# Two modulation vectors by one-column products on TensorE in the opening of a two-block network, with the small vectors loaded ahead on the same queue

## The chip, the cores and the metric

The kernel runs on one core of a Trainium2 chip, in one launch. The metric is the device time of that launch in microseconds (us): the median of the runs shown, 2753.62 us for the kernel before (3 runs, 2752.54 to 2756.70 us).

## The reference, cut to what matters

The first block has two layers, each of attention and a gated feed-forward part, over 1024 tokens of width 1024; a second block follows. Every layer of the first block is modulated by six vectors made from a condition `c`:

```
cond = jax.nn.silu(c)                                   # 1 x 1024
mod = (cond @ ada_w[i] + ada_b[i])                      # 1 x 6144, float32
sh1, sc1, g1, sh2, sc2, g2 = jnp.split(mod, 6, axis=-1)
h = rmsnorm(x, norm_mix[i]) * (1 + sc1) + sh1
y = windowed_gqa(h, a_w_in[j], a_w_out[j], a_sink[j])   # begins with h @ a_w_in
```

For layer 0, `sc1` (vector 1) and `sh1` (vector 0) are needed before the first product `h @ a_w_in`. Each is a product of the 1024 values of `cond` with a 1024 x 1024 block of `ada_w`, 4.2 MB in float32. The change concerns how these two are made; nothing else of the reference is touched.

## The kernel before, in words

Activations are kept transposed: 128 features on the partitions, 512 tokens (a half, `hf`) along the free side, eight feature tiles `j`. A 1024-wide vector lies as 128 partitions x 8 columns.

The opening is written out in `build` (L1961 onwards). `load_vectors` loads nine small vectors: eight go as rows into two buffers through ACT's queue (L207), are transposed on PE (L210) and copied by DVE (L212); the attention sink goes by ACT's queue as well (L239). `cond` is made from the first (L232 to L236). SP's queue then loads, in program order, four 512 KB tiles of x (first half, L303), eight 512 KB blocks of the weights of vector 1 (`w1`, L259), four tiles of x (second half), eight blocks of the weights of vector 0 (`w0`), and after them the first two column blocks of `a_w_in` (three transfers at L544, 512 KB of memory for each block, of which the first is cut in two pieces of 64 columns). The spills of x to memory (L321, eight of 512 KB) and the third column block follow.

On the engines other than SP the order inside `with net.in_order()` is that of the program text, for each engine by itself. For PE it is: 32 transposes of x's first half (`turn_x`, L312), the spreading of the reciprocal norms of that half over 128 partitions (`spread`, L389), the finish of vector 1 (`ada_fin`, eight transposes, L281), 32 transposes of the second half, its spreading, the finish of vector 0, and then the first product of the attention's projection (`project_first`, L590 to L592), which is outside the `with`. ACT squares the rows of x (L494), copies the transposes out of PSUM (L314), and makes the high part of h (`hh`, L527), with vector 0 as its bias. DVE makes the modulation vectors: `ada_acc` runs over the eight blocks of a vector and adds `block * cond[:, k]` to a 128 x 1024 sum (L269 for the first block, L271 for seven); then `ada_fin` transposes the sum on PE and DVE adds up each group of 128 (L282) and adds the bias (L283). DVE also makes the reciprocal square roots by a chain of tiny operations (`rstd_steps`, L335 to L342), scales x by norm and vector 1 (`nu`, L516), and makes the low part of h (`hl`, L530). For vector 0 the program weaves the steps of `ada_acc` with the reciprocal roots of the second half. The two column blocks of `a_w_in` are split into a high part by ACT (L536) and a low part by POOL (L537).

A product of two float32 operands (not rounded to the PE's one-pass format) shows as two LDWEIGHTS and two MATMULs in the trace: `col_sums` (L378) issues four one-column products for each sum, and eight instructions appear for them; `spread` issues four, and eight appear. A transpose shows as one.

Of the kernel before, what the change touches and what calls it, by code (L numbers as in the profile page):

```python
# [15 lines left out]
AX = mybir.AxisListType  # L16

P = 128
L = 1024
D = 1024  # L20
KT = D // P
# [127 lines left out]
class Net:  # L149
# [49 lines left out]
    def load_vectors(self):  # L199
        nc, I = self.nc, self.I  # L200

        def rows(specs, name):
            n = sum(r for _, r in specs)
            raw = self.slab("tmp", shape=(P, 1024))
            at = 0
            for ap, r in specs:
                nc.scalar.dma_start(raw[at:at + r, 0:P], ap)  # L207
                at += r
            ps = self.bank("r")
            nc.tensor.transpose(ps[:, 0:n], raw[0:n, 0:P], self.ident[0:n, 0:n])  # L210
            col = self.cst([P, n], name)
            nc.vector.tensor_copy(col, ps[:, 0:n])  # L212
            return col

        v1 = rows([(I["c"].rearrange("b (r p) -> (b r) p", p=P), 8),
                   (I["ada_b"].rearrange("l (r p) -> (l r) p", p=P), 96)], "v1")
        v2 = rows([(I["norm_mix"].rearrange("l (r p) -> (l r) p", p=P), 16),
                   (I["norm_ffn"].rearrange("l (r p) -> (l r) p", p=P), 16),
                   (I["final_norm"].rearrange("(r p) -> r p", p=P), 8),
                   (I["norm_gain_2"].rearrange("l (r p) -> (l r) p", p=P), 8),  # L220
                   (I["conv_w_2"].rearrange("l k (r p) -> (l k r) p", p=P), 12),
                   (I["b_glu_2"].rearrange("l (r p) -> (l r) p", p=P), 4)], "v2")
        self.c_col = v1[:, 0:8]
        self.adab = v1[:, 8:104]
        self.nmix = v2[:, 0:16]
        self.nffn = v2[:, 16:32]
        self.fnorm = v2[:, 32:40]
        self.ngain2 = v2[:, 40:48]
        self.convw = v2[:, 48:60]
        self.bglu = v2[:, 60:64]  # L230
        th = self.small([P, 8], "cth", 1)
        nc.scalar.activation(th, self.c_col, AF.Tanh, scale=0.5)  # L232
        self.cond = self.cst([P, 8], "cond")
        t2 = self.small([P, 8], "cth2", 1)
        nc.vector.scalar_tensor_tensor(t2, th, 1.0, self.c_col, op0=ALU.add, op1=ALU.mult)
        nc.vector.tensor_scalar_mul(self.cond, t2, 0.5)  # L236
        self.mod = {}
        sinkb = self.cst([P, 16], "sinkb")
        nc.scalar.dma_start(sinkb, I["a_sink"].to_broadcast([P, 16]))  # L239
        self.sink8 = self.cst([P, 16], "sink8")  # L240
        nc.vector.tensor_scalar_mul(self.sink8, sinkb, 8.0)
# [32 lines left out]
    def ada_fin(self, i, v, acc):  # L274
        nc = self.nc
        col = self.cst([P, 8], f"mod{i}_{v}")
        red = self.small([P, 8], "adar")
        for hf in range(2):
            ps = self.bank(self.ada_tag, shape=(P, 4, P))
            for j in range(4):  # L280
                nc.tensor.transpose(ps[:, j, :], acc[:, (hf * 4 + j) * P:(hf * 4 + j + 1) * P], self.ident)  # L281
            nc.vector.reduce_sum(red[:, hf * 4:(hf + 1) * 4], ps, axis=AX.X)  # L282
        nc.vector.tensor_add(col, red, self.adab[:, i * 48 + v * 8:i * 48 + v * 8 + 8])  # L283
        self.mod[i, v] = col
        return col

    def ada_scale(self, i, v, gain):
        col = self.mod[i, v]
        s = self.cst([P, 8], f"sc{i}_{v}")
        self.nc.vector.scalar_tensor_tensor(s, col, 1.0, gain, op0=ALU.add, op1=ALU.mult)  # L290
        return s
# [1669 lines left out]
def build(tc, I, out, dbg=None, stop=None):  # L1961
    with ExitStack() as ctx:
        net, nc = Net(tc, I, out, dbg), tc.nc
        net.open(ctx)
        net.consts()
        net.load_vectors()
        xd, xd1 = net.spill_tile(), net.spill_tile()
        x0 = net.load_x(0)
        w1 = [net.ada_load(0, 1, k, "slab") for k in range(KT)]
        x1 = net.load_x(1)  # L1970
        w0 = [net.ada_load(0, 0, k, "slab") for k in range(KT)]
        net.x = Act(net, "x")
        with net.in_order():
            h, half = net.norm(net.x, lambda v: net.mod[0, 0] if v else s, rows=(x0, x1))
            first, second = Steps(half(0)), Steps(half(1))
            first.run(4)
            net.turn_x(0, x0)
            first.run(12)
            acc = net.ada_acc(w1)
            net.ada_fin(0, 1, acc)  # L1980
            s = net.ada_scale(0, 1, net.nmix[:, 0:8])
            first.run(1)
            second.run(4)
            net.turn_x(1, x1)
            acc = None
            for k in range(KT):
                acc = net.ada_acc(w0[:k + 1], acc, k)
                if k < 6:
                    second.run(2)
            for n, parts in enumerate(([(1024, 64), (1280, 64)], [(0, P)])):  # L1990
                net.ready[n] = net.load_cols(I["a_w_in"][0], parts, eng=nc.gpsimd)
            net.ada_fin(0, 0, acc)
            first.run()
            second.run()
        net.pending = second
        for hf in range(2):
            net.spill_x(xd, hf)
        net.half = {}

        def ffn_norm(i):  # L2000
            s2 = net.ada_scale(i, 4, net.nffn[:, 8 * i:8 * i + 8])
            net.H, half = net.block_norm(net.x, lambda v: net.mod[i, 3] if v else s2, lambda hf: net.spill_x(xd, hf))
            return half

        def b_norm():
            s = net.ada_scale(1, 1, net.nmix[:, 8:16])
            net.h, half = net.norm(net.x, lambda v: net.mod[1, 0] if v else s, ("s", "slab"))

            def both(hf, order=range(KT)):
                for n, _ in enumerate(half(hf, order)):  # L2010
                    if n == KT - 1:
                        net.spill_x(xd1, hf)
                    yield
            return both

        net.layer_a(h, lambda: net.reload_x(xd, True), lambda: ffn_norm(0))
        if stop == "A":
            return net.dump_x()
        early, late = net.ssm_params()
        net.ada_tag = "o"  # L2020
        d = net.ffn_wide(0, net.H, Steps(net.adas([(1, 1), (1, 0), (1, 2), (1, 4), (1, 3)], "wl")))
        net.ffn_narrow(0, d, xd, b_norm, early)
        if stop == "F0":
            return net.dump_x()
        net.layer_b(net.h, lambda: net.reload_x(xd1), lambda: ffn_norm(1))
        if stop == "B":
            return net.dump_x()
        d = net.ffn_wide(1, net.H, Steps(net.adas([(1, 5)], "wl")))
        net.ffn_narrow(1, d, xd, net.mix_norm, late)
        if stop == "F1":  # L2030
            return net.dump_x()
        net.mixer2()
# [41 lines left out]
```

## Time and profile before

| | |
|---|---|
| median of 3 runs | 2753.62 us |
| profiled execution: time, span | 2757.76 us, 2756.0 us |
| PE busy | 2593.1 us (94% of the span) |
| DVE, ACT, POOL busy | 69%, 47%, 14% |
| first main product on PE (L590) begins | 55.70 us |
| PE busy in 0 to 50 us | 15.9 us |
| DMA share in 10 to 50 us | 0.98 to 1.03 |

All times of rows are us from the span's start. The profiled execution is 4.1 us above the median, and 1.8 us of its time lie outside the span. "Granted clock" (PEclk) is the share of TensorE's full 2.4 GHz: 1.00 is that level and 0.50 is 1.2 GHz; a mean over a stretch lies between. Before 19.61 us the profile has no record of it and prints 1.00.

### The profile page before, as it was taken

Reading aid. Unit: us, or ns where it says so; the run is one execution under the profiler, and the core shown is the slowest. Engines: PE = TensorE matmul, PEld = TensorE weight load, DVE = VectorE, ACT = ScalarE, POOL = GpSimd, SP = SyncE. Lnnn points to the kernel's source line nnn. Section 1 sums busy time; section 2 is a strip of 40 time slices with the busy share of each in tenths; the row PEclk is TensorE's granted clock in tenths of the full one; section 3 lists DMA queues with packets and bytes.
Section 4 is the critical chain, followed back from the end, with each engine's and each line's share of the span. In section 5 each row is a group of like instructions: output and inputs, shape, how many; then the busy total and the mean of one; then the engine's idle time right before and its main releaser. Section 6 shows DMA issues by size and latency. Waiting matters only on the chain. (4 is left out here: it accounts for less than half of the span.)

```text
span 2756.0 us, 33954 instructions
## 1 busy us (share of the span) xinstructions
PE 2593.1 (94%) x11966; PEld 2115.1 (77%) x11966; DVE 1899.1 (69%) x3559; ACT 1286.1 (47%) x2416; POOL 376.4 (14%) x506
## 2 busy tenths in 40 slices
PE   4999998999999999988899889999999899999998
PEld 4777676888888788776787668888887777988877
DVE  7788777977775976755667798666656978165355
ACT  4577743433333345568888443333333445123131
POOL 2255521000000000023343200000000102020000
PEclk8999999999999999999999999999999999999999
DMA  7333341544444666311122414222274565161141
GB/s 276 99 93 96 119 123 69 156 142 146 138 138 139 232 200 194 107 39 40 39 55 78 145 59 146 82 86 83 85 244 150 176 199 175 54 180 52 46 144 63
DMA packets 283403, 336.74 MB, mean 122 GB/s; under 512 B 59384, under 2 KB 212704, under 8 KB 282592
## 3 DMA queue, kind: packets, MB, share of 16 engines
q1 hardware_dynamic: 277520, 315.59, 36.4%
q0 software_dynamic: 5312, 18.88, 2.1%
q8 instruction: 94, 1.54, 0.2%
q14 instruction: 77, 0.63, 0.1%
q10 hardware_dynamic: 400, 0.09, 0.0%
HBM read 265.14 MB, written 67.27 MB: 121 GB/s over the span
## 5 line engine op out<-in xcount | busy, mean ns | idle before, releaser
L1188 PE MATMUL psg<-H,wpart 128*128 128x512 f32 x2112 | 504.6, 393 | 14.3 <-ACT H L432 10.0
L1188 PEld LDWEIGHTS psg<-H,wpart 128*128 128x128 f32 x2112 | 397.8, 189 | 103.6 <-ACT H L432 12.8
L1175 ACT CAST wpart<-wraw 128x512 fp32r<-128x512 f32 x264 | 163.3, 622 | 248.3 <-PE pstp L1188 76.4
L1188 PE MATMUL pssc<-H,wpart 128*128 128x512 f32 x1056 | 255.0, 390 | 0.5 <-DVE ev L1208 0.5
L1188 PEld LDWEIGHTS pssc<-H,wpart 128*128 128x128 f32 x1056 | 198.1, 188 | 42.1 <-DVE ev L1208 0.9
L1176 DVE TENSOR_TENSOR wpart<-wraw,wpart 128x512 fp32r<-128x512 f32 x264 | 180.9, 686 | 68.5 <-ACT wpart L1175 66.7
L1325 PE MATMUL psg<-part,wpart 128*128 128x512 f32 x792 | 206.8, 394 | 8.0 <-DVE wpart L1291 3.1
L1325 PE MATMUL pssc<-part,wpart 128*128 128x512 f32 x792 | 207.4, 394 | 5.2 <-DVE ev L1212 3.6
L590 PE MATMUL psg<-hh,wh 128*128 128x512 f32 x480 | 198.5, 414 | 2.2 <-ACT hh L527 1.7
L1290 ACT CAST wpart<-wraw 128x640 fp32r<-128x640 f32 (+1 forms) x132 | 101.0, 765 | 210.7 <-PE psg L1325 101.8
L591 PE MATMUL psg<-hl,wh 128*128 128x512 f32 x480 | 192.6, 401 | 2.0 <-DVE hl L530 1.9
L592 PE MATMUL psg<-hh,wl 128*128 128x512 f32 x480 | 191.8, 400 | 0.0
L1325 PEld LDWEIGHTS psg<-part,wpart 128*128 128x128 f32 x792 | 148.4, 189 | 42.7 <-DVE part L1297 5.5
L126 ACT ACTIVATE s<-s,nm 128x256 f32<-128x256 f32 (+4 forms) x320 | 162.4, 511 | 39.6 <-DVE nm L122 33.1
L1325 PEld LDWEIGHTS pssc<-part,wpart 128*128 128x128 f32 x792 | 148.3, 189 | 39.4 <-DVE ev L1212 4.3
L1291 DVE TENSOR_TENSOR wpart<-wraw,wpart 128x640 fp32r<-128x640 f32 (+1 forms) x132 | 117.7, 892 | 83.4 <-ACT wpart L1290 75.8
L1203 ACT COPY ev<-psg 128x512 f32<-128x512 f32 x132 | 77.4, 588 | 205.1 <-PE psg L1188 141.0
L780 POOL TENSOR_TENSOR o<-o,ob 64x512 f32<-64x512 f32 x80 | 117.3, 1467 | 231.8 <-ACT o L779 221.6
L403 POOL TENSOR_TENSOR nacc<-nacc,nsq 128x512 f32<-128x512 f32 x30 | 40.5, 1350 | 761.8 <-ACT nsq L401 761.5
L1325 PE MATMUL pstp<-part,wpart 128*128 128x512 f32 x528 | 137.9, 393 | 0.0
L1296 ACT CAST part<-a 128x512 fp32r<-128x512 f32 x176 | 108.5, 618 | 58.0 <-PE pssc L1325 17.7
L1297 DVE TENSOR_TENSOR part<-a,part 128x512 fp32r<-128x512 f32 x176 | 119.6, 691 | 19.0 <-ACT part L1296 17.8
(454 smaller groups left out, 5488.8 us busy)
## 6 DMA issues: line engine op xcount, KB each, us to landing
adaw<-in_ada_w_dram SPq DMA_DIRECT2D x96, 512.0 KB, 4.2
wraw<-in_ffn_w_in_dram SPq DMA_DIRECT2D x88, 512.0 KB, 3.9
a<-acts SPq DMA_DIRECT2D x132, 256.0 KB, 4.0
acts<-ev SPq DMA_DIRECT2D x44, 512.0 KB, 2.7
wraw<-in_ffn_w_out_dram SPq DMA_DIRECT2D x44, 384.0 KB, 3.5
xs<-x SPq DMA_DIRECT2D x32, 512.0 KB, 3.5
x<-xs SPq DMA_DIRECT2D x32, 512.0 KB, 5.1
wraw<-in_ffn_w_out_dram SPq DMA_DIRECT2D x44, 320.0 KB, 3.3
```

The source lines that it names most:

```text
L126: self.net.nc.scalar.activation(s[:, 0:w], s[:, 0:w], AF.Exp, bias=self.nm[:, i:i + 1], scale=0.125, accum_out=self.l[:, i:i + 1])
L590: nc.tensor.matmul(ps, hi[:, k, :], xhi, start=(k == 0), stop=False)
L591: nc.tensor.matmul(ps, hi[:, k, :], xlo, start=False, stop=False)
L592: nc.tensor.matmul(ps, lo[:, k, :], xhi, start=False, stop=(k == KT - 1))
L780: nc.gpsimd.tensor_add(oap, oap, b)
L1175: nc.scalar.copy(t[:, lo_half], src)
L1176: nc.vector.tensor_sub(t[:, hi_half], src, fl(t[:, lo_half]))
L1188: nc.tensor.matmul(bank[q, key], a[:, ks], b, start=first and k == m == 0, stop=k == 3 and m == 2, skip_group_check=not first)
L1291: nc.vector.tensor_sub(lo, t[:, 0:n], fl(hi))
L1296: nc.scalar.copy(o[:, lo_half], a)
L1297: nc.vector.tensor_sub(o[:, hi_half], a, fl(o[:, lo_half]))
L1325: nc.tensor.matmul(banks[m], a[:, ms], b, start=k == n == 0, stop=k == NK - 1 and n == 2)
```

## The change

The eight row vectors are issued on SP's queue, ahead of x, instead of ACT's. The three transfers of `a_w_in` are issued ahead of `w0` instead of behind it. `ada_acc` and `ada_fin` give way, for these two vectors, to `ada_mm`: for each block `k` and each of eight 128-column slices `n` of it, the 128 x 128 slice is the stationary operand and one column of `cond` the moving one; the 64 results land in 64 PSUM columns, and one DVE reduction over `k` and one addition finish the vector. The split of the two column blocks stands behind all of the second half's reciprocal roots, and ahead of vector 0.

```
-                nc.scalar.dma_start(raw[at:at + r, 0:P], ap)
+                nc.sync.dma_start(raw[at:at + r, 0:P], ap)
...
+    def ada_mm(self, i, v, raws):
+        nc = self.nc
+        ps = self.bank("r", shape=(P, 8, KT))
+        for k, raw in enumerate(raws):
+            for n in range(8):
+                nc.tensor.matmul(ps[:, n, k:k + 1], raw[:, n * P:(n + 1) * P], self.cond[:, k:k + 1], start=True, stop=True)
+        red = self.small([P, 8], "adar")
+        nc.vector.reduce_sum(red, ps, axis=AX.X)
+        col = self.cst([P, 8], f"mod{i}_{v}")
+        nc.vector.tensor_add(col, red, self.adab[:, i * 48 + v * 8:i * 48 + v * 8 + 8])
+        self.mod[i, v] = col
...
         x1 = net.load_x(1)
+        raw = [net.raw_cols(I["a_w_in"][0], parts) for parts in ([(1024, 64), (1280, 64)], [(0, P)])]
         w0 = [net.ada_load(0, 0, k, "slab") for k in range(KT)]
...
             first.run(12)
-            acc = net.ada_acc(w1)
-            net.ada_fin(0, 1, acc)
+            net.ada_mm(0, 1, w1)
             s = net.ada_scale(0, 1, net.nmix[:, 0:8])
             first.run(1)
             second.run(4)
             net.turn_x(1, x1)
-            acc = None
-            for k in range(KT):
-                acc = net.ada_acc(w0[:k + 1], acc, k)
-                if k < 6:
-                    second.run(2)
-            for n, parts in enumerate(([(1024, 64), (1280, 64)], [(0, P)])):
-                net.ready[n] = net.load_cols(I["a_w_in"][0], parts, eng=nc.gpsimd)
-            net.ada_fin(0, 0, acc)
+            second.run(12)
+            for n in range(2):
+                net.ready[n] = net.split_cols(raw[n], nc.gpsimd)
+            net.ada_mm(0, 0, w0)
             first.run()
             second.run()
```

## Rows read from the trace of the kernel before

**Rows 1.** Busy time of each engine in stretches of 10 us from the start, with the granted clock, the DMA share and what the DMA moved. Columns: the stretch and its length, then for PE, PE's weight loads, DVE, ACT and POOL the busy us and in brackets the instructions; granted clock, DMA share, GB/s.

```profile
0.00:10.00 10.00, 1.58 (x5) 0.86 (x5) 0.14 (x3) 3.03 (x4) 1.71 (x9) 1.00 0.55 177
10.00:20.00 10.00, 5.86 (x29) 5.86 (x30) 6.14 (x24) 6.06 (x14) 3.01 (x8) 1.00 0.98 395
20.00:30.00 10.00, 2.50 (x17) 2.31 (x16) 8.58 (x8) 4.75 (x9) 1.12 (x6) 0.82 1.03 410
30.00:40.00 10.00, 5.42 (x35) 5.19 (x33) 9.59 (x19) 5.00 (x10) 0.30 (x2) 0.84 0.98 337
40.00:50.00 10.00, 0.49 (x2) 0.50 (x3) 9.90 (x12) 2.09 (x2) 5.33 (x2) 0.50 1.00 377
...
60.00:70.00 10.00, 10.00 (x44) 8.26 (x43) 9.82 (x15) 4.75 (x7) 1.42 (x2) 0.97 0.00 0
```

**Rows 2.** The timeline of DVE, POOL and ACT from 31.8 us to the first main product: start, duration, what, and in brackets the idle time before it and what ended it.

```profile
31.78 5.36 DVE L516 SCALAR_TENSOR_TENSOR nu<-x,sc,pso 128x512 f32<-128x512 f32 x8
37.05 0.75 DVE L269 TENSOR_SCALAR tmp<-adaw,cond 128x1024 f32<-128x1024 f32 x1
...
41.70 1.04 ACT L536 CAST wh<-wr 128x1024 fp32r<-128x1024 f32 x1 [5.44 <-DMA wr<-in_a_w_in_dram]
42.11 0.16 DVE L340 TENSOR_TENSOR rs_t<-rs_t,nms 128x4 f32<-128x4 f32 x1
42.31 0.16 DVE L342 SCALAR_TENSOR_TENSOR rs_y<-rs_t,rs_y 128x4 f32<-128x4 f32 x1
...
42.83 5.33 POOL L537 TENSOR_TENSOR wl<-wr,wh 128x1024 fp32r<-128x1024 f32 x2 [11.77 <-ACT wh L536]
43.58 2.30 DVE L338 SCALAR_TENSOR_TENSOR rs_t<-rs_y 128x4 f32<-128x4 f32 x1
45.92 2.27 DVE L340 TENSOR_TENSOR rs_t<-rs_t,nms 128x4 f32<-128x4 f32 x1
49.41 2.61 DVE L271 SCALAR_TENSOR_TENSOR tmp<-adaw,cond,tmp 128x1024 f32<-128x1024 f32 x2
53.23 1.46 DVE L282 TENSOR_REDUCE adar<-psg 128x4 f32<-128x512 f32 x2 [1.21 <-PE psg L281]
54.73 0.17 DVE L283 TENSOR_TENSOR mod<-adar,v 128x8 f32<-128x8 f32 x1
54.93 5.01 ACT L527 ACTIVATE hh<-nu,mod 128x512 fp32r<-128x512 f32 x8 [10.61 <-DVE mod L283]
```

**Rows 3.** The timeline of PE in the same opening: the first half's transposes and spreading, the finish of vector 1, transposes of the second half, its spreading, and the first main products.

```profile
14.14 0.48 PE L312 MATMUL pssc<-ident,xraw 128*128 128x128 f32 x1 [4.23 <-DMA xraw<-in_x_dram]
...
16.97 1.06 PE L312 MATMUL pssc<-ident,xraw 128*128 128x128 f32 x4
17.82 1.06 PE L312 MATMUL pstp<-ident,xraw 128*128 128x128 f32 x4
...
20.01 1.06 PE L389 MATMUL pso<-ident,rs_y 128*128 128x128 f32 x8
28.57 1.97 PE L281 MATMUL psg<-ident,tmp 128*128 128x128 f32 x8 [7.50 <-DVE tmp L271]
...
33.95 0.60 PE L312 MATMUL pstp<-ident,xraw 128*128 128x128 f32 x4
34.39 0.60 PE L312 MATMUL pssc<-ident,xraw 128*128 128x128 f32 x4
49.51 2.07 PE L389 MATMUL pso<-ident,rs_y 128*128 128x128 f32 x8 [14.08 <-DVE rs_y L342]
55.70 0.74 PE L590 MATMUL psg<-hh,wh 128*128 128x512 f32 x2 [1.74 <-ACT hh L527]
```

**Rows 4.** The one-column products that the kernel before has, in the timeline of PE: eight instructions (four products) between main products, and sixteen (eight products) ahead of transposes.

```profile
430.93 0.95 PE L378 MATMUL pssc<-ones,nacc 128*128 128x1 f32 x8
431.74 0.49 PE L576 MATMUL pstp<-oh,wohi 128*128 128x512 f32 x1
...
2321.71 1.95 PE L378 MATMUL pstp<-ones,nacc 128*128 128x1 f32 x16 [1.17 <-POOL nacc L1677]
2323.51 1.88 PE L1729 MATMUL pstp<-ident,x 128*128 128x128 f32 x8
```

**Rows 5.** Stretches of the opening that begin and end where the granted clock is recorded anew (columns as in the first group).

```profile
19.61:23.02 3.41, 1.46 (x13) 1.27 (x11) 3.34 (x3) 1.07 (x2) 0.00 (x0) 1.00 1.03 411
...
26.44:29.85 3.41, 1.28 (x6) 1.29 (x7) 2.17 (x3) 3.02 (x7) 1.12 (x6) 0.50 1.03 411
29.85:33.27 3.42, 3.42 (x18) 3.42 (x17) 3.08 (x7) 2.16 (x5) 0.30 (x2) 0.50 1.03 410
33.27:36.68 3.41, 2.15 (x20) 1.92 (x18) 3.41 (x6) 2.99 (x6) 0.00 (x0) 1.00 1.02 401
36.68:40.09 3.41, 0.00 (x0) 0.00 (x0) 3.34 (x8) 0.00 (x0) 0.00 (x0) 1.00 0.89 197
40.09:43.51 3.42, 0.00 (x0) 0.00 (x0) 3.35 (x7) 1.29 (x2) 0.68 (x1) 0.50 0.97 306
```

**Rows 6.** The same for PE alone around the sixteen one-column instructions (busy, granted clock, DMA share, GB/s).

```profile
2320.20:2323.61 3.41, 2.24 (x20) 1.00 0.86 296
2323.61:2327.02 3.41, 3.41 (x18) 0.50 0.12 50
```

**Rows 7.** The loads of the opening. First and last of the eight vectors' issues on ACT's queue (minimum, median and maximum of the issue's own time in ns, its start), then SP's issues (start, time from the first to the end of the last, count), what held SP's x loads up (us in total, times, longest), and the time from issue to landing of the x loads.

```profile
L207 ACTq DMA_DIRECT2D tmp<-in_c_dram x1: 583/583/583, 0.8 to 0.8; - x1
...
L207 ACTq DMA_DIRECT2D tmp<-in_b_glu_dram x1: 255/255/255, 6.3 to 6.3; - x1
...
0.81 6.11 SPq L303 DMA_DIRECT2D xraw<-in_x_dram  x4
...
30.77 8.80 SPq L544 DMA_DIRECT2D wr<-in_a_w_in_dram  x3
...
SPq L303 <- DMA xraw<-in_x_dram: 2.9, 1, 2.9
...
SPq L303 <- DMA tmp<-in_norm_ffn_dram: 1.6, 1, 1.6
...
DMA to landing us min/median/max: 3.8/4.8/10.2
```

## The prediction

> **What bounds the kernel now.** I read the page's busy shares first: PE is busy 94% of the span, so a change of a few instructions shows only where PE waits. The stretches of 10 us come next, for they show where that is: in the first 50 us PE is busy 15.9 us (1.58 + 5.86 + 2.50 + 5.42 + 0.49), while DMA runs at about 400 GB/s from 10 us on and DVE is busy 8.6 to 9.9 us of every 10 from 20 to 50 us [rows 1]. From 60 us on PE is full. So the opening is worth what moves the first main product, L590 at 55.70 us [rows 3]; everything behind it waits for it, and the rest of the kernel is PE-bound, so I carry a shift of that instant one to one to the end.
>
> The timeline of DVE then tells what L590 waits for [rows 2]. ACT makes `hh` after DVE's addition at 54.73 us, that follows the reductions, those the transposes, and those the last `ada_acc` step, which ends at 52.0 us. DVE works from 37.05 us without a rest: eight steps, the tiny root operations between them, and two of these that take 2.30 and 2.27 us, while POOL makes `wl` for 5.33 us, where the two before them take 0.16 us. The end of the opening is DVE's, not DMA's.
>
> **The change part by part.**
>
> *Removed.* DVE loses two times 0.75 + 7 x 1.28 = 9.7 us of `ada_acc`, four reductions and, on the path, the two stretched root operations; PE loses two finishes of eight transposes (1.97 us for one [rows 3]). All of DVE's wait in front of L590 goes. What is late next is then PE, as follows.
>
> *Vectors first.* Eight issues go onto SP ahead of x. The eight issues took 0.26 to 0.58 us on ACT's queue, 0.38 us on average [rows 7], so x's first goes out at 0.8 + 8 x 0.38 = 3.9 us instead of 0.81 us. Before, x's last tile landed at 14.1 us (PE waits for it until 14.14 us [rows 3]): the first 10 us moved only 177 GB/s [rows 1], since SP issued its first four transfers over 6.11 us [rows 7], held up 1.6 us for one of the vectors and 2.9 us for an earlier tile [rows 7]. With the vectors out of the way I take the shortest landing, 3.8 us [rows 7], for the first tile, and 512 KB at 410 GB/s = 1.28 us for each of the other three: 3.9 + 3.8 + 3 x 1.28 = 11.5 us, 2.6 us earlier. Bounds: 10.3 us (one transfer time less) and 17.1 us (all of the 3 us lost).
>
> *First half on PE.* From the landing to the end of the spreading PE needed 14.14 to 21.07 us, 6.9 us, before [rows 3]; nothing in that changes: 11.5 + 6.9 = 18.4 us.
>
> *The products.* A vector has 8 x 8 = 64 products, and each is two instructions: the four products of a column sum show as eight [rows 4]. Eight step in 431.74 - 430.93 = 0.81 us, sixteen in 2323.51 - 2321.71 = 1.80 us [rows 4]: 0.1125 us each at the granted clock of 1.00. So a vector costs PE 128 x 0.1125 = 14.4 us, and a block (eight products) 1.8 us against 1.28 us to load it: PE, not DMA, sets the pace. No one-column product stands at the low clock. There, transposes step four in 0.855 us, 0.214 us each, against 0.44 us for four at 1.00 [rows 3], and the spreading takes 2.07 us for what takes 1.06 us. So at 0.50 a vector costs up to 128 x 0.214 = 27.4 us.
>
> Which clock? It rose at 19.61 us, 5.5 us after PE had begun its transposes in earnest, and fell at 26.44 us when PE had been idle since 21.07 us; it rose again at 33.27 us and was at 0.50 from 40.09 us [rows 5]. Whether one-column products hold it up is the open question, and two stretches answer: between 33.27 and 36.68 us PE was busy 2.15 us with transposes, and the clock stayed 1.00; between 2320.20 and 2323.61 us it was busy 2.24 us, of which sixteen one-column instructions made 1.8 us, and behind it stood 0.50 [rows 5, 6]. I take it that they don't hold the clock. Then a stretch of products begins at full clock behind the transposes, and loses it. Before, the high clock lasted 6.8 us from 19.61 us, of which transposes and spreading took 1.5 us; it may end sooner under work of this kind, so I take 5 us: 22 products at 0.225 us, and 42 at 0.428 us = 18.0 us. A vector is 23.0 us, near the upper bound; the ends 14.4 and 27.4 us stay for the range.
>
> *The chain.* On PE the order is fixed, so all of it adds up. Vector 1: 18.4 + 23.0 = 41.4 us; its last block landed long before (12 transfers after 11.5 us would be 26.9 us even with x's second half). The second half's 32 transposes now stand behind these products instead of in a gap: 5.5 us at 0.214 us and the last six at 0.11 us are 6.2 us, with the spreading 0.9 us: 48.5 us. Vector 0: 71.5 us; its blocks, 1 MB later in the queue, have landed by about 41 us (worked out with the third rival). Then the last product's own 0.3 us, a reduction of 64 elements (0.69 us for 512 is the upper bound, 0.16 us, DVE's smallest operations [rows 2], the lower: 0.25 us), and the addition to L590 as before, 54.73 to 55.70 us, 0.97 us [rows 2, 3]: 73.0 us. That is 17.3 us later than 55.70 us. The main products then start at the low clock; before they had about 3 us of it, after perhaps 5 us, which adds 1.0 us. Sum: 18.3 us.
>
> *Edits at nothing.* The move of the `a_w_in` transfers ahead of `w0`, and the split on ACT (2 x 1.04 us) and POOL (5.33 us [rows 2]) behind the second half's copies, are hidden under vector 0's products (they would be over by about 56 us, against 73 us); so are the spills and the third column block behind them on SP, about 10 and 3 us of DMA after 48 us. With less cover (the clock kept, x's copies over at about 37 us) the split would end at about 45 us, and still ahead of that case's L590. `nu` (5.4 us of DVE) lies under the products as well. The reductions wait at the head of DVE's queue with only `nu` or `hl` behind them, which need their result anyway.
>
> Two rules of the Trainium skill would give another sum. For steps the rows say 0.1125 us an instruction. The skill ("TensorE: Matmul & The Clock Gate", section "Back-to-back issue gap") has matmuls of 1 to 64 columns follow each other at about 25 ns; by that a vector would be an estimated 3.2 us and the DMA would set the end. The rows here, where every product brings new weights, don't agree. For the clock, the rows show it rising behind transposes alone [rows 5]. The same page (section "Part 4: PE-mode transpose") says that transposes don't count as PE being busy; by that the clock would be low throughout. The rows don't agree with that either.
>
> **The rivals.**
>
> *The products keep the clock up.* Then a vector is 14.4 us: 18.4 + 14.4 + 3.5 (32 transposes at 0.11 us) + 0.9 + 14.4 + 1.5 = 53.1 us, 2.6 us earlier than before: 2751.0 us, no change. For it: PE is never idle in this chain, and every one-column instruction seen ran at 1.00 [rows 4]. Against: what stood behind sixteen of them [rows 6].
>
> *The clock stays low throughout*, as when the transposes between the products don't lift it: 19.4 + 27.4 + 6.8 + 2.1 + 27.4 + 1.5 = 84.6 us, 28.9 us later: 2782.5 us. Against it: both rises of rows 5 came behind transposes.
>
> *DMA sets the end, faster than before.* If a block's products take no longer than its 1.28 us (0.16 us a product; this decides), L590 follows the last block of `w0`: 26.9 us + 4 us for `a_w_in` (1 MB would be 2.6 us at 410 GB/s, SP took 8.8 us to issue it before [rows 7]; nearer the first, as other transfers are still queued) + 8 x 1.28 us = 41.1 us, and 3 us for its products and the finish: 44 us, 11.7 us earlier, 2742 us. This is what the removal of DVE's 20 us would give. Against it: 0.225 us a product [rows 4].
>
> *It doesn't do what it says*, that is, the products wait for blocks: no, for PE comes to the blocks of either vector after they have landed.
>
> **How the numbers follow.** Chances: clock lost behind the transposes 0.68, kept 0.20, low throughout 0.08, DMA sets the end 0.04. The likeliest gives 2757.76 + 18.3 = 2776.1 us for the profiled execution, which stands 4.1 us above the median; on the median, 2753.62 + 18.3 = 2771.9 us. Its own range is 2763 us (the clock comes back for half of the products) to 2779 us. The range 2750 to 2781 us takes in the kept clock's 2751.0 us and nearly all of the low one. About 0.2% (5.5 us) is what a measurement of this kernel can tell from no change. Faster: the DMA case and a fifth of the kept clock, where x lands at 10.3 us and all transposes go at full clock (another 4 us), 0.08; within: the rest of the kept clock, 0.16; slower: 0.76.
>
> **What would show it.** In the profile after: x's last tile lands at 11 to 12 us; two groups of 128 one-column MATMULs, the first beginning at 18 us; their granted clock 1.00 at the beginning and 0.50 for the greater part; PE nearly gapless from 12 us to L590, and L590 at about 73 us; DVE mostly idle in the opening. Wrong would be: products at 0.1125 us throughout (L590 at 53 us), products fewer than two instructions each, or gaps in which PE waits for a block.

## The result, and the profile after

The changed kernel takes 2788.06 us (median of 4 runs, 2786.86 to 2790.15 us) where the kernel before takes 2755.16 us in the runs beside it: a ratio of 1.0122, 95% interval 1.0105 to 1.0139. That is 1.2% slower. The direction was forecast with 0.76; the size was not: 2772 us was forecast, and the time lies above the range, whose end was 2781 us.

| | before | after |
|---|---|---|
| profiled execution: time, span | 2757.76, 2756.0 us | 2787.47, 2785.8 us |
| x's last tile of the first half on PE | 14.14 us | 12.36 us |
| first main product on PE | 55.70 us | 84.35 us |
| from there to the end of the time | 2702.1 us | 2703.1 us |

The last two rows say where the 29.7 us of the profiled pair went: 28.65 us are lost before the first main product (L603 now, L590 before), 1.06 us behind it. The timeline of PE after shows the opening, as [rows 3] did for before. Lines are start, duration, what, and in brackets the idle time before and what ended it; L325 are the transposes, L402 the spreading, L293 the new products.

```profile
12.36 0.47 PE L325 MATMUL pssc<-ident,xraw 128*128 128x128 f32 x1 [0.80 <-DMA xraw<-in_x_dram]
...
17.05 1.06 PE L402 MATMUL pso<-ident,rs_y 128*128 128x128 f32 x8
17.94 23.40 PE L293 MATMUL pssc<-cond,adaw 128*128 128x1 f32 x128
41.20 1.09 PE L325 MATMUL pstp<-ident,xraw 128*128 128x128 f32 x4
...
46.68 0.60 PE L325 MATMUL pssc<-ident,xraw 128*128 128x128 f32 x4
53.75 2.08 PE L402 MATMUL pso<-ident,rs_y 128*128 128x128 f32 x8 [6.47 <-DVE rs_y L355]
55.62 27.31 PE L293 MATMUL pstp<-cond,adaw 128*128 128x1 f32 x128
84.35 1.22 PE L603 MATMUL psg<-hh,wh 128*128 128x512 f32 x2 [1.43 <-ACT hh L540]
```

Read from top to bottom it is one chain on PE, with a single hole: 6.47 us in front of the second spreading, for which DVE's roots (L355) are late. Each vector is 128 instructions, and the two vectors take 23.4 and 27.3 us, 50.7 us together, where the kernel before needed PE for 16 transposes.

The same stretches by busy time and granted clock (columns as in [rows 5]), cut where the clock is recorded anew and where the second vector begins and ends:

```profile
15.40:22.23 6.83, 6.83 (x64) 6.83 (x63) 0.23 (x2) 2.56 (x5) 0.00 (x0) 1.00 1.02 413
22.23:46.12 23.89, 23.89 (x114) 23.89 (x114) 4.54 (x10) 7.31 (x13) 1.21 (x8) 0.50 1.01 362
46.12:49.53 3.41, 1.16 (x11) 0.93 (x9) 3.10 (x13) 3.29 (x6) 0.50 (x1) 1.00 1.02 418
49.53:55.60 6.07, 1.85 (x8) 1.85 (x9) 4.13 (x2) 0.36 (x1) 4.14 (x2) 0.50 0.84 288
55.60:82.96 27.36, 27.33 (x130) 27.24 (x128) 0.00 (x0) 0.00 (x0) 0.00 (x0) 0.50 0.07 16
```

PE is busy without a gap from 22.23 to 46.12 us, and from 55.60 to 82.96 us, and the granted clock is 0.50 in both. The clock rises twice, both times behind transposes (before 15.40 us the profile of this run has no record and prints 1.00; four transposes step 0.85 us there, as they do at 0.50 from 41.20 us on). In the last stretch nothing else runs: DVE, ACT and POOL stand at 0.00, and the DMA moves 16 GB/s.

What the hole hides is in the timeline of DVE, POOL and ACT:

```profile
29.62 0.18 ACT L507 ACTIVATION_READ_ACCUMULATOR nsq<-xraw 128x1 f32 x1
...
42.13 5.36 DVE L529 SCALAR_TENSOR_TENSOR nu<-x,sc,pso 128x512 f32<-128x512 f32 x8
47.41 0.16 DVE L514 TENSOR_SCALAR nms<-nss 128x4 f32<-128x4 f32 x1
...
48.98 0.16 DVE L351 SCALAR_TENSOR_TENSOR rs_t<-rs_y 128x4 f32<-128x4 f32 x1
49.03 4.64 POOL L550 TENSOR_TENSOR wl<-wr,wh 128x1024 fp32r<-128x1024 f32 x2 [18.86 <-ACT wh L549]
49.18 2.21 DVE L353 TENSOR_TENSOR rs_t<-rs_t,nms 128x4 f32<-128x4 f32 x1
...
51.43 2.27 DVE L355 SCALAR_TENSOR_TENSOR rs_y<-rs_t,rs_y 128x4 f32<-128x4 f32 x1
```

The roots of the second half begin at 47.41 us, though ACT had squared and summed the last rows of x by 29.8 us (L507): in DVE's order they stand behind `nu`, which needs vector 1. Their last two operations take 2.21 and 2.27 us instead of 0.16 us, while POOL makes `wl`. In [rows 2] two operations of the same chain are as long beside POOL, on DVE's path; the prediction counted them as removed, and the change has put them on PE's path.

### The profile page after: what moved, and what is told of

Its sections match the earlier page's. It is cut to its first block, busy times and chain, and to the rows that moved or that the text cites. A ratio compares the mean times of both kernels' runs of the same rounds, so it can differ in the third digit from the quotient of the medians.

```text
span 2785.8 us, 34415 instructions
## 1 busy us (share of the span) xinstructions
PE 2644.5 (95%) x12206; PEld 2164.8 (78%) x12206; DVE 1871.6 (67%) x3541; ACT 1284.9 (46%) x2416; POOL 377.2 (14%) x506
## 5 line engine op out<-in xcount | busy, mean ns | idle before, releaser
L603 PE MATMUL psg<-hh,wh 128*128 128x512 f32 x480 | 200.2, 417 | 1.9 <-ACT hh L540 1.4
L1310 DVE TENSOR_TENSOR part<-a,part 128x512 fp32r<-128x512 f32 x176 | 120.1, 694 | 22.9 <-ACT part L1309 21.7
```

Source lines behind the costliest of these rows:

```text
L603: nc.tensor.matmul(ps, hi[:, k, :], xhi, start=(k == 0), stop=False)
L1310: nc.vector.tensor_sub(o[:, hi_half], a, fl(o[:, lo_half]))
```

## The experiments

Ten kernels ran. The first group changes one thing of the kernel before or of the changed kernel; the second puts parts together. "First" is the start of the first main product in the profile; each ratio is to runs of the kernel before made beside that run (medians of 2753.48 to 2755.16 us). There is one profile for each kernel, and the place where the clock changes differs between them: the 128 one-column products of vector 1 took 22.59, 23.40 and 25.16 us in three of them, so a difference of 2 us in "first" proves little.

| run | median us | ratio to before, 95% interval | first |
|---|---|---|---|
| change | 2788.06 | 1.0122 [1.0105, 1.0139] | 84.35 us |
| vectors only | 2751.35 | 0.9992 [0.9979, 1.0005] | 52.49 us |
| roots first | 2770.98 | 1.0068 [1.0048, 1.0088] | 74.88 us |
| split on DVE | 2777.67 | 1.0097 [1.0078, 1.0115] | 77.92 us |
| 128 columns | 2767.56 | 1.0049 [1.0030, 1.0067] | 64.54 us |
| 32 columns | 2784.23 | 1.0107 [1.0091, 1.0124] | 83.55 us |
| 128 columns, roots first | 2751.52 | 0.9995 [0.9984, 1.0005] | 53.36 us |
| loads only | 2753.71 | 0.9996 [0.9987, 1.0006] | 53.94 us |
| shared | 2756.11 | 1.0016 [1.0004, 1.0027] | 52.42 us |
| shared, vector 0's blocks first | 2745.32 | 0.9973 [0.9962, 0.9984] | 47.18 us |
| the same, roots first | 2744.87 | 0.9966 [0.9953, 0.9978] | 45.46 us |

**The vectors alone.** Edit, in the kernel before:

```
-                nc.scalar.dma_start(raw[at:at + r, 0:P], ap)
+                nc.sync.dma_start(raw[at:at + r, 0:P], ap)
```

> The kernel before, with one line of the change: the eight small vectors on SP's queue ahead of x. Theory: this part is a gain. x's last tile lands at about 12.4 us as in the changed kernel (14.1 us before), the DVE chain of the modulation vectors starts about 2 us earlier, and the first main product begins at 53 to 54 us instead of 55.7: 2 us faster, about 2753 us where the kernel before has 2755. Rival: eight issues in front of x on one queue cost their own 3 us, and the first main product begins at 57 to 58 us.

PE's timeline of this run:

```profile
11.93 0.47 PE L312 MATMUL pssc<-ident,xraw 128*128 128x128 f32 x1 [0.81 <-DMA xraw<-in_x_dram]
...
52.49 0.79 PE L590 MATMUL psg<-hh,wh 128*128 128x512 f32 x1 [1.74 <-ACT hh L527]
```

x's first half is complete on PE 2.2 us earlier than before, and the first main product comes 3.2 us earlier. The runs' ratio is 0.9992, and its interval holds 1: the gain in the opening is plain in the trace and too small to be told in the time of the whole kernel. No cost of this part of the change shows.

**The roots ahead of the scaling.** Edit, in the changed kernel:

```
-            s = net.ada_scale(0, 1, net.nmix[:, 0:8])
-            first.run(1)
             second.run(4)
             net.turn_x(1, x1)
+            net.spread_tag = "g"
             second.run(12)
+            net.spread_tag = "o"
+            s = net.ada_scale(0, 1, net.nmix[:, 0:8])
+            first.run(1)
```

> The changed kernel, with the second half's reciprocal roots put ahead of the scaling of the first half in DVE's order, and the second half's spreading in a PSUM buffer of its own, so that it need not wait for that scaling. Theory: what the prediction left out is the 6.5 us that PE stands still between the second half's transposes and its spreading (47.2 to 53.75 us); without it the spreading follows at about 47 us, the clock is still at 1.00 when vector 0's products begin, and these take 23 to 24 us like vector 1's instead of 27.3. First main product at 73 to 75 us instead of 84.35, about 10 us faster than the changed kernel. Rival: the products lose the clock anyway, and only the wait goes: 77 to 78 us.

PE's timeline around the second spreading, then two stretches with the granted clock:

```profile
49.34 0.60 PE L325 MATMUL pssc<-ident,xraw 128*128 128x128 f32 x4
49.77 1.06 PE L402 MATMUL psg<-ident,rs_y 128*128 128x128 f32 x8
50.67 22.94 PE L293 MATMUL pstp<-cond,adaw 128*128 128x1 f32 x128
74.88 0.80 PE L603 MATMUL psg<-hh,wh 128*128 128x512 f32 x1 [1.27 <-ACT hh L540]
```

```profile
48.76:55.59 6.83, 6.83 (x64) 6.83 (x62) 3.37 (x6) 3.79 (x6) 3.90 (x2) 0.99 0.63 244
55.59:74.88 19.29, 18.02 (x85) 17.93 (x86) 0.41 (x3) 0.77 (x2) 1.78 (x3) 0.50 0.21 51
```

The hole is gone, the clock is still up when vector 0's products begin, and they take 22.9 us. The first main product stands at 74.88 us where the prediction had 73.0 us, and the whole is 2771 us where it had 2772 (vector 1, 25.16 us in this profile, is 2.2 us above its term). So the prediction had timed this kernel, which has neither the late roots nor what follows from them.

**POOL's part in the stretched roots.** Edit, in the changed kernel:

```
-                net.ready[n] = net.split_cols(raw[n], nc.gpsimd)
+                net.ready[n] = net.split_cols(raw[n], nc.vector)
```

> The changed kernel, with the low parts of the two column blocks made by DVE instead of POOL, behind the second half's roots. Theory: two of the root operations take 2.21 and 2.27 us because POOL works on SBUF beside them; with POOL idle they take 0.16 us, the spreading follows at 49.5 us instead of 53.75, and the first main product begins at about 80 us: 4 us faster than the changed kernel, or up to 8 if the clock then lasts into the products. Rival: the stretched operations wait for something else (the scaling in front of them, SBUF traffic of the DMA); then they stay, and the two subtractions on DVE change nothing.

DVE's timeline, then PE's:

```profile
48.38 0.16 DVE L353 TENSOR_TENSOR rs_t<-rs_t,nms 128x4 f32<-128x4 f32 x1
48.57 0.16 DVE L355 SCALAR_TENSOR_TENSOR rs_y<-rs_t,rs_y 128x4 f32<-128x4 f32 x1
48.68 2.36 DVE L550 TENSOR_TENSOR wl<-wr,wh 128x1024 fp32r<-128x1024 f32 x2
```

```profile
48.79 1.16 PE L402 MATMUL pso<-ident,rs_y 128*128 128x128 f32 x8 [3.15 <-DVE rs_y L355]
49.78 26.71 PE L293 MATMUL pstp<-cond,adaw 128*128 128x1 f32 x128
```

The same two operations take 0.16 us each when POOL is idle, and DVE does POOL's 4.64 us in 2.36 us. PE's wait falls from 6.47 to 3.15 us, and the first main product comes 6.4 us earlier: 4.2 us for the two stretched operations (2.21 + 2.27 - 2 x 0.16), 0.8 us because vector 1 happened to take 22.59 us here, and 1.5 us because the spreading and the first of vector 0's products still found the clock at 1.00. The scaling in front of the roots is the same and the DMA no less busy (a share of 1.02 from 45.64 to 48.79 us), so the rival is refuted. The Trainium skill ("SBUF — State Buffer", section "Who interferes with whom") says that a DVE instruction with two SBUF inputs and a GpSimd instruction that reads SBUF exclude each other for the whole of an instruction; the traces agree, with 2.21 and 2.27 us beside POOL's two operations of 2.3 us. The rows show it for operations with one SBUF input as well: in the run with 128 columns, which comes next, POOL makes `wl` from 38.24 to 42.88 us, and the stretched operations are the first two of the chain:

```profile
38.80 1.81 DVE L514 TENSOR_SCALAR nms<-nss 128x4 f32<-128x4 f32 x1
40.64 2.26 DVE L348 TENSOR_SCALAR rs_y<-nms 128x4 int32<-128x4 int32 x1
```

**The width of the moving operand.** Edit, in the changed kernel (with 32 for `P` in the other run), the sum over `k` then taking the first 64 columns:

```
-        ps = self.bank("r", shape=(P, 8, KT))
+        ps = self.bank("r", shape=(P, 64 + P))
...
-                nc.tensor.matmul(ps[:, n, k:k + 1], raw[:, n * P:(n + 1) * P], self.cond[:, k:k + 1], start=True, stop=True)
+                nc.tensor.matmul(ps[:, 8 * k + n:8 * k + n + P], raw[:, n * P:(n + 1) * P], self.cond[:, k:k + 1].to_broadcast([P, P]), start=True, stop=True)
```

> The changed kernel, with each product's moving operand widened from one column of cond to 128 copies of it; of the 128 result columns the first is kept, the others are overwritten. Same weights, same loads, same number of instructions. Theory: the price of a product is that of the granted clock, which one-column products don't hold up; with 128 columns the clock stays at 1.00 behind the first transposes, an instruction steps 0.11 us, a vector takes 14.4 us instead of 23.4 and 27.3. First main product at about 63 us (84.35 - 9 - 13), 2767 us. Rival: the products step 0.213 us because their weights are read while the DMA writes SBUF, or because 128 weight columns take that long whatever the clock; then more moving columns give no gain, and the first main product stays at 84 us or comes later.

> The changed kernel with 32 moving columns instead of 128, everything else as in the run with 128. It measures how the price goes between one column and 128. Theory (the clock follows what PE does): the first stretch of products is nearer the 23.4 us of one column than the 14.5 us of 128, with the clock falling back to 0.50 in it. Rival (weights loads run slowly beside the DMA unless the moving side is long): the step changes in between without the granted clock changing, for instance 18 us at a clock that stays at 1.00.

PE's timeline with 128 columns, and its stretches of products once the clock is up:

```profile
18.27 14.46 PE L293 MATMUL pssc<-cond,adaw 128*128 128x128 f32 x128
...
44.72 2.08 PE L402 MATMUL pso<-ident,rs_y 128*128 128x128 f32 x8 [8.50 <-DVE rs_y L355]
46.59 16.52 PE L293 MATMUL pstp<-cond,adaw 128*128 128x128 f32 x128
64.54 0.73 PE L603 MATMUL psg<-hh,wh 128*128 128x512 f32 x2 [1.43 <-ACT hh L540]
```

```profile
18.27:32.50 14.23, 14.23 (x130) 14.23 (x129) 0.00 (x0) 4.60 (x8) 1.21 (x8) 1.00 1.01 334
...
51.04:63.00 11.96, 11.96 (x109) 11.88 (x107) 0.00 (x0) 0.00 (x0) 0.00 (x0) 1.00 0.43 121
```

And with 32 columns:

```profile
17.09 23.31 PE L293 MATMUL pssc<-cond,adaw 128*128 128x32 f32 x128
...
54.77 27.36 PE L293 MATMUL pstp<-cond,adaw 128*128 128x32 f32 x128
```

```profile
21.53:40.30 18.77, 18.77 (x90) 18.77 (x90) 0.00 (x0) 4.59 (x8) 1.21 (x8) 0.50 1.01 340
54.77:82.10 27.33, 27.33 (x129) 27.22 (x128) 0.00 (x0) 0.00 (x0) 0.00 (x0) 0.50 0.08 16
```

With 128 times the moving columns vector 1 takes 14.46 us instead of 23.40, at a granted clock of 1.00 throughout, from the same weights, in the same number of instructions, beside the same DMA traffic. That rules out the reading of the weights beside the DMA as the reason; vector 0's one-column products step as slowly at a DMA share of 0.07. Vector 0 runs its first 4.5 us at 0.50, behind the hole (8.50 us here), and the rest at 1.00, and the first main product comes at 64.54 us, where about 63 us was expected. The run with 32 columns behaves as the one with a single column: 23.3 and 27.4 us, at 0.50 from 21.53 us on in the first vector and throughout in the second. The price is 0.113 us an instruction (two for each product) at 1.00 and 0.213 us (27.31 / 128) at 0.50; neither the width of the moving operand nor the DMA traffic moves it in these runs.

**Both repairs.** The edits of the two runs above together.

> The changed kernel with both repairs: 128 moving columns, and the second half's roots ahead of the scaling with a PSUM buffer of its own for the spreading. Theory: what is left is PE's own chain at 1.00: 18.3 + 14.5 + 3.6 for the transposes + 0.9 + 14.5 + 1.5 = 53.3 us for the first main product, 2 us ahead of the 55.7 us of the kernel before, about 2753 us: no gain, as 14.4 us is the floor of such a vector on PE. Rival: the two repairs overlap (the clock was lost in the wait alone), and the sum is no better than with the wide products, 64 us.

```profile
18.80 14.46 PE L293 MATMUL pssc<-cond,adaw 128*128 128x128 f32 x128
...
36.58 1.06 PE L402 MATMUL psg<-ident,rs_y 128*128 128x128 f32 x8
37.48 14.46 PE L293 MATMUL pstp<-cond,adaw 128*128 128x128 f32 x128
53.36 0.73 PE L603 MATMUL psg<-hh,wh 128*128 128x512 f32 x2 [1.43 <-ACT hh L540]
```

53.36 us, to 0.1 us as expected, with both vectors at 14.46 us and no wait of PE between 18 us and the end of the products. The two costs add up: the roots alone gave 9.5 us, the columns alone 19.8 us, both together 31.0 us of the opening. What remains, 28.9 us of products on PE, brings the first main product 2.3 us ahead of the kernel before and 0.9 us behind the run with the vectors alone, which has DVE's accumulation; the ratio is 0.9995, no change.

**The loads and the order without the products.** Edit, in the changed kernel:

```
-            net.ada_mm(0, 1, w1)
+            net.ada_fin(0, 1, net.ada_acc(w1))
...
-            net.ada_mm(0, 0, w0)
+            net.ada_fin(0, 0, net.ada_acc(w0))
```

> The changed kernel with its order of loads and of the opening, but the two vectors made on DVE as before. It tells what the change's moves are worth without its products. Theory: the moves gain, and all of the loss is the products': DVE makes vector 1 by 26 us, scales until 34 us, then takes the blocks of vector 0 as they land behind the a_w_in transfers, the last at about 44 us: first main product at about 50 us, 5 us ahead of before. Rival: the moves cost too (vector 0's blocks come 6 us later, and POOL's splitting now falls on DVE's accumulation): 55 us or later.

DVE's timeline:

```profile
36.82 2.27 DVE L355 SCALAR_TENSOR_TENSOR rs_y<-rs_t,rs_y 128x4 f32<-128x4 f32 x1
...
40.18 0.74 DVE L269 TENSOR_SCALAR tmp<-adaw,cond 128x1024 f32<-128x1024 f32 x1
40.96 9.21 DVE L271 SCALAR_TENSOR_TENSOR tmp<-adaw,cond,tmp 128x1024 f32<-128x1024 f32 x7
```

53.94 us: later than the expected 50 us, and 1.4 us later than with the vectors alone, though earlier than before. DVE is the bound again: stretched roots come first, and the eight blocks then go in one piece until 50.2 us, without a wait for a block. So the moves of the column blocks and of their split gain or cost nothing that the times can tell (0.9996), and the change's loss comes with the products, in the order in which they stand. The rival was right in part: POOL's splitting falls on the roots, not on the accumulation, and the result lies between the two.

**Sharing the vectors between DVE and PE.** DVE adds up the first blocks (`nd` of them), PE takes the others, and the sum of DVE is one more block with ones as the moving operand; 128 columns; the split on DVE.

```
+        acc = self.ada_acc(raws[:nd])
+        terms = [(raws[k], self.cond[:, k:k + 1]) for k in range(nd, KT)] + [(acc, self.ones)]
...
+        for k, (raw, c) in enumerate(terms):
+            for n in range(8):
+                nc.tensor.matmul(ps[:, 8 * k + n:8 * k + n + P], raw[:, n * P:(n + 1) * P], c.to_broadcast([P, P]), start=True, stop=True)
```

> A version that shares the work: DVE multiplies and adds the first four blocks of each vector, PE takes the other four and the sum (with ones as the moving operand), all with 128 moving columns; the low parts of the column blocks on DVE; loads in the changed kernel's order. Theory: PE needs 5 x 1.8 = 9 us for a vector, beside 4.6 us of DVE, and the end is then set by the last block of vector 0, which lands at about 44 us behind the a_w_in transfers: first main product at 47 to 49 us, 7 to 8 us ahead of the kernel before, about 2747 us. Rival: PE's chain still sets it, with gaps for blocks in which the clock falls: 52 us or later, no difference from before.

> The same sharing with the a_w_in transfers behind vector 0's blocks again, as in the kernel before, five of vector 0's blocks on DVE, and the second column block's low part made after the first half's h. Theory: the order of these loads is nearly indifferent, for the first main product needs both; vector 0 is done at about 43 us, the first column block lands at about 40 us and is split by 43.5 us: first main product at 44 to 46 us, about 10 us ahead of before, 2745 us. Rival: the column block's landing and split end last, 48 us or later, and then the order of the changed kernel is the better one.

> The shared version with vector 0's blocks loaded first, and in addition the second half's roots ahead of the scaling with a PSUM buffer of its own for the spreading, and four of vector 0's blocks on DVE instead of five. Theory: the spreading no longer waits for the roots (4.1 us of PE's wait in the version before), PE takes the blocks as they land until about 39 us, DVE's sum is done at about 41 us, and the first main product begins at 44 to 45 us instead of 47.2: 2 to 3 us more, about 2743 us. Rival: the landing and splitting of the first column block (43.1 us) ends last: 46 to 47 us, no difference from the version before.

PE's timeline of the first of these, with a stretch of it, and PE's timeline of the last:

```profile
36.38 2.08 PE L406 MATMUL pso<-ident,rs_y 128*128 128x128 f32 x8 [4.36 <-DVE rs_y L359]
39.12 10.26 PE L295 MATMUL pstp<-cond,adaw 128*128 128x128 f32 x64 [0.67 <-DMA adaw<-in_ada_w_dram]
```

```profile
39.12:49.22 10.10, 10.10 (x64) 10.10 (x65) 4.03 (x4) 0.00 (x0) 0.00 (x0) 0.70 1.02 414
```

```profile
32.22 1.06 PE L406 MATMUL psg<-ident,rs_y 128*128 128x128 f32 x8
35.04 7.38 PE L295 MATMUL pstp<-cond,adaw 128*128 128x128 f32 x64 [1.76 <-DMA adaw<-in_ada_w_dram]
42.26 1.95 PE L295 MATMUL pstp<-ones,tmp 128*128 128x128 f32 x16
45.46 0.50 PE L607 MATMUL psg<-hh,wh 128*128 128x512 f32 x1 [1.25 <-ACT hh L544]
```

The first misses, 52.4 us instead of 47 to 49, and its runs show no gain (1.0016): the roots behind `nu` make PE wait 4.36 us, the clock is at 0.50 behind that, and four blocks take 10.3 us at a mean clock of 0.70. The second has vector 0's blocks loaded first, five of them on DVE, and the second low part made later; it reaches 47.2 us, later than the 44 to 46 us expected, and which of its three edits brings how much was not separated. With the roots first in addition, and four blocks on DVE, the last reaches 45.46 us, just past its 44 to 45 us, the four blocks on PE in 7.4 us. The last two are faster than both kernels, by 0.3%: 0.9973 and 0.9966, with intervals below 1. The step between them, 1.7 us in the opening, is not told apart by their times.

That the sharing does this, and not the split taken off POOL, is not shown by a run of its own. An estimate from the run with the loads only: 53.94 us less 4.1 us for its two stretched operations (2.19 and 2.27 us, instead of 0.16) plus 2.4 us for the split on DVE is 52.2 us with DVE alone, 5 to 7 us behind the last two.

## Why the prediction was right or wrong

*Right: what the path is.* It said that with DVE's work gone PE's own chain sets the end, that a product is two instructions at 0.1125 us and PE never waits for a block, that the one-column products don't hold the clock, and that the opening's shift carries to the end. Vector 1's term was 23.0 us and measured 23.4. The end of vector 1 was set at 41.4 us and lies at 41.34, but so close an agreement is luck: x's last tile came 0.9 us later than the 11.5 us of the sum, and PE went from there to the end of the first spreading in 5.6 us instead of 6.9 (12.36 to 17.94), as the clock rose at 15.40 us in the middle of the transposes. Behind the first main product the kernel after takes 1.06 us more, where 1.0 was said. The reason given is in the trace, for the main products begin with 6.1 us at 0.50 (84.35 to 90.50) instead of 3.4; but the agreement in size proves nothing, since this remainder lies between 2695 and 2705 us over all kernels here, which have the same work there. By the clock records of the traces, the clock stands at 0.50 for 84 us of it in the kernel with the shortest remainder (roots first) and for 100 us in the one with the longest (the last of the table); no run tests whether that is the cause.

*Right in direction: the vectors.* x landed 1.8 us earlier instead of 2.6; the run with this part alone shows a first main product 3.2 us earlier.

*Wrong: the second spreading.* The step that failed is "with the spreading 0.9 us: 48.5 us": I let it follow the transposes, as if its input were ready. It begins at 53.75 us instead of 47.6. The sentence on DVE's queue was wrong too, that the reductions have "only `nu` or `hl` behind them": the second half's roots stand there as well, and `nu` in front of them. In the kernel before they were late too (PE waits 14.08 us for them in [rows 3]), but vector 0 was later still, and so the wait cost nothing there. The split was called hidden under vector 0's products; its cover was counted for POOL, but not for the roots beside it, and the two stretched operations stood under *Removed*, though the roots that they belong to stay on DVE.

*Wrong by consequence: vector 0.* Its 23.0 us assumed the high clock behind the transposes. In the hole the clock fell back, and it took 27.3 us, the upper bound of its term.

The sum of the misses, from the two timelines: 6.15 us for the late start of the spreading (53.75 - 47.6), 1.0 us for the spreading at the low clock, 4.3 us for vector 0, less 0.1 us in the rest, make 11.35 us, which is 84.35 - 73.0. The run with the roots first takes all of it away but 1.9 us.

*The rivals.* "The products keep the clock up" (53.1 us) is refuted by both long stretches at 0.50; a clock that does stay up, with 128 columns and early roots, gives 53.36 us. "The clock stays low throughout" comes nearest by number, 84.6 us, but not by its mechanism: the clock rose behind the transposes both times. The range ended where it did since it was drawn around one stall-free chain and its two clocks; a wait for DVE inside that chain was in none of the cases.

## What to carry to other kernels

When work moves from one engine to another, follow the old engine's queue as well as the new one's: what stood harmlessly behind a late instruction may now be on the path, and it is found by asking for each input of the new chain where its producer stands in its engine's order. A wait on TensorE is paid twice when the work behind it then starts at the low clock: here 6.5 us of waiting, and vector 0 in 27.3 us instead of the 22.9 us of the run with the roots first. A matrix times a vector on TensorE, with the matrix as the stationary side, cost the same step for each instruction with 1, 32 and 128 moving columns at the same clock; widening to 128 columns was free here and kept the clock. Sharing the blocks between two engines gave the two fastest kernels, with loads and roots in a fitting order; in the changed kernel's order it gave nothing.

## What was not expected of the hardware

An instruction with 128 moving columns steps no slower than one with a single column when each brings new 128 x 128 float32 weights (0.113 us at 1.00 for both: [rows 4] and 14.46 us / 128), and it is faster in effect because the granted clock stays at 1.00. PE can be busy without a gap for 27.3 us, as the profile counts it, at a granted clock of 0.50 from beginning to end. And DVE made the low parts of the two column blocks in 2.36 us, for which POOL took 4.64 us while stopping DVE.
